# Two heads in row halves of TensorE, and a 32x32 block inverse in 32x32 array tiles, in the middle phase of an encoder layer

## The chip, the cores and the metric

One Trainium2 chip, one core. The metric is device time in microseconds of one launch of the whole layer; lower is better. The core has a matrix engine (TensorE, PE in the profile, with PEld for its weight loads), VectorE (DVE), ScalarE (ACT), GpSimd (POOL), SyncE (SP, which issues transfers here) and 16 DMA engines.

## The reference, cut to what matters

One encoder layer runs on two groups of tokens, 2048 and 256 long, with width 1024. Half of the heads are attention heads (8 of 64 columns), half are RWKV-7 heads (8 of 64), and a feed-forward part follows.

```python
h = rmsnorm(x, g_norm1) * (1.0 + sc1) + sh1
p = h @ w_in
attn = attention_mixer(p[..., :ATTN_IN], ...)      # dilated windows (128,1), (512,4), (2048,16)
rw = rwkv7_mixer(p[..., ATTN_IN:], ...)            # forward + backward scan
x = x + gt1 * (concat([attn, rw]) @ w_out)
x = x + gt2 * (square(relu(h2 @ w_ff1)) @ w_ff2)
...
def _rwkv_step(state, inp):
    w, kk, b, k, v, r = inp
    sa = einsum('dbhvk,dbhk->dbhv', state, kk)
    state = state * w[..., None, :] - sa[..., :, None] * b[..., None, :] + v[..., :, None] * k[..., None, :]
    y = einsum('dbhvk,dbhk->dbhv', state, r)
```

Attention needs, for each block of 128 queries and 128 to 256 keys, the scores `q @ k.T` of each head, a bias, an exponential and the product with the values. The scan is not run token by token: the kernel cuts it into chunks of 64 tokens, and in each chunk a 64x64 triangular matrix (made of products of the keys) has to be inverted before the state can be carried on.

## The kernel before, in words

The layer has three phases. `phase_a` (L292) is the input projection and what prepares the heads, `phase_b` (L1097) holds attention and the scan together, and `phase_c` (L1926) is the output projection with the feed-forward part. The change touches `phase_b` alone, beside two cost functions of the planner that it uses.

**Who sets the order.** In `phase_b` the work is written as generators ("streams"), and a planner, `Pace` (its `drive` is at L243), draws from them one step at a time: always the stream whose next step could begin earliest by an estimate, less a priority. The estimates are cost functions: `pe` (L143) for TensorE, `dve` (L164) for VectorE, with fixed latencies between engines. Only the order of each engine's instructions comes out of it; on the chip each engine runs its own list in that order and waits on semaphores. Where the planner foresees a gap on TensorE it writes filler products into the list (`warm`, L95, called by `heat`, L1123: 384-column f16 products of the constant `bdh` that nobody reads), to keep the granted clock up. All recorded operations pass one helper, so nearly every row of the profile says L117, and rows are told apart by their tiles' names.

**The scan.** Two neighbouring heads share one pass `c` of 128 partitions (head 0 in partitions 0 to 63, head 1 in 64 to 127), and there are four passes. For each pass and direction `d` (0 forward, 1 backward), 36 chunks are taken in "units" of eight (the short sequence: of four), 40 units in all. For a unit:

- `load_stream` (L1178) loads `kr` and `bk`. `prod_stream` (L1190) makes the key products: for four chunks at a time and one head after the other, a product over that head's 64 partitions, four chunks of head 0 into one PSUM bank `pb`, four of head 1 into another. `mask_stream` (L1212) copies them to SBUF as `x`, `gate_stream` masks them.
- `unit_prep` (L1294) inverts. The two diagonal 32x32 blocks of each head's 64x64 matrix are inverted together (four blocks for the two heads), as one block-diagonal 128x128 matrix per chunk: five levels, each one or two f16 products for every chunk of the unit, then one refinement and the off-diagonal block in split precision (`h` and `l` are the high and the low f16 part). Its left operands must be 128x128 with zeros off the diagonal: the copies `e`, `eof` live in zeroed tiles (`e32`, `eof`), and `spread` (L1313) is a VectorE multiply of a compact 128x(chunks x 32) tile by a mask into a 128x1024 tile (`mb`, `mbl`). `prep_stream` (L1857) runs one unit per direction at a time.
- `late_load` (L1239) and `late_gate` (L1252) bring the rest for half a unit: `rc`, the values into `uv`, and the transposed, weighted `bk` (which stays in SBUF from the first load until then).
- `pair_chain` (L1425) is the recurrent chain, 144 steps (4 passes x 36 chunks), both directions and both heads in one step. Each step runs five groups of four products on TensorE (`pc`), with ACT (`rr`, `uv`), POOL (`sw`) and DVE (`uv`) between them.

**Attention.** `attention` (L1561) cuts each pass into 50 blocks, 200 in all. `block` (L1601) yields a job: scores into a PSUM bank `ps` (two banks), a VectorE pass `p<-ps,tb` per head that adds the bias and takes the minimum, exponential on ACT, transposes `pt`, product with values into `pb`. Both heads' scores come from one product over all 128 partitions: the keys stand in `kz` (L1173), which has one half per head with the other head's partitions zeroed, so 2 x 256 columns are moved. For the windows of dilation 4 and 16 the keys and queries are read with that stride. At most six blocks are in flight.

PSUM has eight banks here: three `pb`, two `ps`, two `pc`, one `pt`.

## Time and profile before

| | us |
|---|---|
| median of 3 runs (4226.86 to 4237.39) | 4229.41 |
| the profiled execution | 4239.46 |
| its span, first to last instruction | 4237.6 |
| `phase_a`, until the first `pb` product | 0 to 1073 |
| `phase_b` | 1073 to 2361 |
| `phase_c` | 2361 to 4238 |

Two things help in reading it. An f32 product leaves two records in the trace (an f32 transpose and an f16 product one), so "x8" of `pb<-kr,bk` are four products. And a record's duration contains the way through the array, about 170 to 270 ns that overlap with the records behind it; what a product costs its neighbours is read from start to start in the timeline.

### The profile page before, as it was taken

How to read it: one execution, taken by the hardware profiler on the slowest of the kernel's cores; microseconds unless marked ns; L12 is line 12 of the kernel's file. 1: busy time of each engine (PE TensorE's matmuls, PEld its weight loads, DVE VectorE, ACT ScalarE, POOL GpSimd, SP SyncE). 2: the span in 40 equal slices, each digit the busy share in tenths (PEclk: the TensorE clock that was granted, in tenths of full speed). 3: DMA queues.
4: the chain of work that ended last, by engine and by line, in shares of the span. 5: the costliest groups of instructions: out<-in, count | busy, mean ns of one | idle time of the engine just before them, and what ended most of it. 6: DMA issues, size and time to landing. Idle time of an engine off the chain costs nothing.

```text
span 4237.6 us, 76554 instructions
## 1 busy us (share of the span) xinstructions
PE 4035.7 (95%) x29994; PEld 3339.5 (79%) x29994; DVE 2606.8 (62%) x5429; ACT 1754.5 (41%) x4301; POOL 1484.1 (35%) x1471
## 2 busy tenths in 40 slices
PE   8989999998899999999999799999999999999997
PEld 5878789888566666666666588889999888889997
DVE  4898788788668768767667354444444464444445
ACT  5556556555565566566465322121221221112221
POOL 2553431211645645645544443112121141112123
PEclk9999999999899899899799899999999999999999
DMA  6566565454433323324222444111111141111112
GB/s 228 205 224 224 173 201 191 152 171 153 145 79 94 106 69 93 110 71 109 83 75 55 155 145 154 41 40 48 42 44 42 53 167 40 40 40 43 48 41 80
DMA packets 341674, 452.57 MB, mean 107 GB/s; under 512 B 152384, under 2 KB 237376, under 8 KB 340288
## 3 DMA queue, kind: packets, MB, share of 16 engines
q1 hardware_dynamic: 340480, 446.98, 32.8%
q8 instruction: 236, 3.87, 0.4%
q14 instruction: 126, 1.03, 0.1%
q10 hardware_dynamic: 832, 0.69, 0.1%
HBM read 319.90 MB, written 127.68 MB: 106 GB/s over the span
## 4 chain that ended last, share of the span: by engine, by line
PE 54%; DVE 4%; issue 1%; ACT 1%; POOL 1%; DMA 0%; POOLq 0%; SPq 0%; DVEq 0%; ACTq 0%
PE p L117 42%; PE pb L117 5%; PE pc L117 3%; PE ps L117 3%; PE pt L117 1%; DVE mb L117 1%; DVE m L117 0%; DMA mx<-scr_mix 0%; DVE uv L117 0%; DVE mc L117 0%; DVE t L117 0%; POOL ya L117 0%; POOL x L117 0%; DVE w L117 0%; DVE p L117 0%
## 5 line engine op out<-in xcount | busy, mean ns | idle before, releaser
L117 DVE TENSOR_TENSOR z<-z 128x384 f32<-128x384 f32 x192 | 190.2, 991 | 591.1 <-ACT gh L117 591.1
L117 DVE TENSOR_TENSOR ya<-ya,p 128x512 f32<-128x512 f32 x540 | 363.9, 687 | 277.5 <-PE p L117 276.5
L117 PE MATMUL pin<-hi,whi 128*128 128x386 f32 (+3 forms) x1512 | 499.4, 330 | 16.6 <-ACT praw L325 8.9
L117 PE MATMUL p<-hi,mh 128*128 128x384 f32 x1536 | 513.3, 334 | 0.0
L117 PE MATMUL p<-hi,ml 128*128 128x384 f32 x1536 | 513.2, 334 | 0.0
L117 PE MATMUL p<-lo,mh 128*128 128x384 f32 x1536 | 513.0, 334 | 0.0
L117 PE MATMUL pin<-hi,wlo 128*128 128x386 f32 (+3 forms) x1512 | 484.6, 320 | 6.3 <-POOL wlo L117 5.1
L117 PE MATMUL pin<-lo,whi 128*128 128x386 f32 (+3 forms) x1512 | 484.0, 320 | 1.2 <-DVE lo L117 1.2
L117 PE MATMUL p<-xn,gh 128*128 128x512 f32 x1152 | 458.9, 398 | 0.0
L117 PE MATMUL p<-mx,gh 128*128 128x512 f32 x1152 | 458.1, 398 | 0.5 <-DVE ya L117 0.5
L117 PE MATMUL p<-mx,gl 128*128 128x512 f32 x1152 | 452.1, 392 | 0.0
L117 POOL TENSOR_TENSOR xn<-x,mx 128x1024 fp32r<-128x1024 f32 x64 | 152.8, 2407 | 653.7 <-ACT mx L117 653.7
L117 ACT ACTIVATE mx<-x 128x1024 fp32r<-128x1024 f32 x64 | 64.3, 1052 | 694.6 <-PE p L117 694.6
L117 POOL TENSOR_TENSOR ml<-x,mh 128x1024 fp32r<-128x1024 f32 x64 | 153.8, 2403 | 556.1 <-ACT mh L117 556.1
L117 PEld LDWEIGHTS pin<-hi,whi 128*128 128x128 f32 x1512 | 292.2, 193 | 30.3 <-ACT praw L325 9.8
L117 PEld LDWEIGHTS pin<-hi,wlo 128*128 128x128 f32 x1512 | 292.6, 193 | 9.3 <-POOL wlo L117 7.0
L117 PEld LDWEIGHTS pin<-lo,whi 128*128 128x128 f32 x1512 | 293.3, 194 | 5.5 <-DVE lo L117 2.7
L117 PEld LDWEIGHTS p<-hi,mh 128*128 128x128 f32 x1536 | 288.3, 188 | 1.5
L117 PEld LDWEIGHTS p<-lo,mh 128*128 128x128 f32 x1536 | 288.3, 188 | 1.3
L117 PEld LDWEIGHTS p<-hi,ml 128*128 128x128 f32 x1536 | 288.3, 188 | 0.0
L117 PE MATMUL ps<-kz,q 128*128 128x512 f32 (+2 forms) x400 | 272.7, 775 | 0.8 <-DVE st L117 0.6
L117 PEld LDWEIGHTS p<-mx,gh 128*128 128x128 f32 x1152 | 215.8, 187 | 56.5 <-DVE ya L117 0.9
(303 smaller groups left out, 8895.8 us busy)
## 6 DMA issues: line engine op xcount, KB each, us to landing
x<-wff SPq DMA_DIRECT2D x128, 512.0 KB
whi<-scr_wp SPq DMA_DIRECT2D x54, 512.0 KB
wlo<-scr_wp SPq DMA_DIRECT2D x54, 512.0 KB
raw<-wada SPq DMA_DIRECT2D x83, 256.0 KB
scr_kr<-kr SPq DMA_DIRECT2D x48, 384.0 KB
scr_bk<-bk SPq DMA_DIRECT2D x48, 384.0 KB
x<-xp SPq DMA_DIRECT2D x32, 512.0 KB
kr<-scr_kr SPq DMA_DIRECT2D x32, 512.0 KB
```

Source lines behind the costliest of these rows:

```text
L117: return f(out, *a, **k)
```

## The change

Six edits, all for `phase_b`:

1. **Key products.** `prod_stream` takes two `pb` banks at once and alternates the heads chunk by chunk, so that each product over partitions 0 to 63 is followed by one over 64 to 127.
2. **Scores.** `kz` loses its zeroed halves. Each head's scores are a product over its own 64 partitions, into a bank of its own, so a block takes both `ps` banks.
3. **Inverse.** `spread` and its masks go. `blocks` makes, for each chunk, four products of 32x32 blocks, block q from partitions 32q to 32q+31 to output partitions 32q to 32q+31 (for the off-diagonal block to those of the other block of the head). The operands stay compact.
4. **Two units in flight** per direction: four `prep` and four `low` streams instead of two, with four sets of tiles; `NX` 6 instead of 5 and `NLATE` 4 instead of 3.
5. **Buffers.** `bk` is dropped after the key products (`NBK` 2), and `late_load` loads it again in halves as `bkl`. In `uv` the head becomes the outer index, and `sw` is two tiles.
6. **The planner's numbers.** Scores and key products count half (`mm2`), a 32-row f16 product n/6 + 2.5 ns, a VectorE transpose at 0.87 elements per ns.

```diff
@@ Pace.pe
-    def pe(self, f):
-        def cost(out, a, b=None, *_, **k):
+    def pe(self, f, share=1.0):
+        def cost(*z, **k):
+            t, c = whole(*z, **k)
+            return t * share, c
...
-                return max(26.0, n / 2.4 + 3), n * rows
+                return (n / 6.0 + 2.5 if m == 32 else max(26.0, n / 2.4 + 3)), n * rows
@@ phase_b
+        mm2 = pace.pe(nc.tensor.matmul, 0.5)
...
-        NKR, NBK, NX, NH, NLATE, NY = 1, 3, 5, 3, 3, 4
+        NKR, NBK, NX, NH, NLATE, NY = 1, 2, 6, 3, 4, 4
...
-        kz = cp.tile([128, 2, NT], FT, name="kz")
-        for hd in range(2):
-            nc.gpsimd.memset(kz[64 - 64 * hd:128 - 64 * hd, hd], 0.0)
+        kz = cp.tile([128, NT], FT, name="kz")
@@ prod_stream
-                    for hd in range(2):
-                        pr = slice(64 * hd, 64 * hd + 64)
-                        yield room("pb", NPB), "P"
-                        ps, turn = pbank([128, 4, 128])
-                        for n in range(4):
-                            mm(ps[:, n], bk[pr, n0 + n, :], kr[pr, n0 + n, :], start=True, stop=True)
...
+                    yield room("pb", NPB), room("pb", NPB - 1), "P"
+                    u[n0, 0], u[n0, 1] = pbank([128, 4, 128]), take(psB, [128, 4, 128], FT, "pb", NPB)
+                    for n in range(4):
+                        for hd in range(2):
+                            pr = slice(64 * hd, 64 * hd + 64)
+                            mm2(u[n0, hd][0][:, n], bk[pr, n0 + n, :], kr[pr, n0 + n, :], start=True, stop=True)
@@ late_load
+                    yield room(f"bkl{d}", 1), "S"
+                    h["bkl", d] = take(su, [128, 4, 128], FT, f"bkl{d}", 1)
+                    dma_(h["bkl", d][0], S["bk"][c, d, :, n0:n0 + 4, :])
@@ unit_prep
-            def spread(c32, mask, name):
-                z = su.tile([128, 8, 128], FH, name=name, bufs=1)
-                tt(z[:, :nn].rearrange("p n (b t) -> p n b t", b=4), c32[:, :nn, None, :].to_broadcast([128, nn, 4, 32]),
-                   mask[:, None].to_broadcast([128, nn, 4, 32]), OP.mult)
-                return z
...
+            def blocks(ps, w, swap, *pairs):
+
+                for n in range(nn):
+                    for z, (a, b) in enumerate(pairs):
+                        for q in range(4):
+                            r, o = slice(32 * q, 32 * q + 32), slice(32 * (q ^ swap), 32 * (q ^ swap) + 32)
+                            mm(ps[o, n, 0:w], a[r, n], b[r, n], start=z == 0, stop=z == len(pairs) - 1)
...
-                    for n in range(nn):
-                        mm(ps[:, n, 0:16], mb[:, n], xs[:, n], start=True, stop=True)
+                    blocks(ps, 16, 0, (mc, xs))
...
                 vtr(fl(mc), fl(t))
-                if li < 4:
-                    mb = spread(mc, bd32, f"mb{d}")
@@ attention, block
-                    yield room("ps", 2), qk
-                    ps, turn = bank([128, 2, 256], "ps", 2)
-                    mm(ps[:, :, :nk], q[:, qs], kz[:, :, ks], start=True, stop=True)
+                    yield room("ps", 2), room("ps", 1), qk
+                    ps, turns = zip(bank([128, 256], "ps", 2), take(psB, [128, 256], FT, "ps", 2))
+                    for hd in range(2):
+                        pr = slice(64 * hd, 64 * hd + 64)
+                        mm2(ps[hd][:, :nk], q[pr, qs], kz[pr, ks], start=True, stop=True)
@@ prep_stream and its call
-            for u in units[d::2]:
+            for u in units[d::4]:
...
-            pace.add(prep_stream(d), "prep", lambda d=d: prog[1, d] + BT["prep"])
-            pace.add(low_stream(d), "low", lambda d=d: prog[1, d] + BT["low"])
+            for k in (d, d + 2):
+                pace.add(prep_stream(k), "prep", lambda d=k: prog[1, d] + BT["prep"])
+                pace.add(low_stream(k), "low", lambda d=k: prog[1, d] + BT["low"])
```

What moves on the engines is read from the order of the instructions. Three places matter. In each row stand the operation, output tile and operands, and the output's shape; the number behind a name is that of the buffer, and "x4" are four equal instructions in a row.

TensorE, the key products of four chunks, before: `pb_15542` takes head 0 and `pb_15552` head 1.

```order
L117 MATMUL pb_15536<-t1_15461,e3201_11132 128x16
L117 MATMUL pb_15542<-kr_15417,bk_15418 128x128 x4
L117 MATMUL pb_15552<-kr_15417,bk_15418 128x128 x4
L117 LDWEIGHTS mb1_15483
L117 MATMUL pb_15564<-xs1_15549,mb1_15483 128x16
```

And now, in the same kind of place (`pb_11698` is head 0, `pb_11699` head 1; behind them follow blocks of the inverse, now 32x16):

```order
L117 MATMUL pb_11660<-xs0_11607,mc0_11566 32x16
L117 MATMUL pb_11698<-kr_11489,bk_11490 128x128
L117 MATMUL pb_11699<-kr_11489,bk_11490 128x128
L117 MATMUL pb_11698<-kr_11489,bk_11490 128x128
L117 MATMUL pb_11699<-kr_11489,bk_11490 128x128
...
L117 LDWEIGHTS e3201_11132
L117 MATMUL pb_11722<-t1_11618,e3201_11132 32x16
```

The heads now alternate (the pair stands four times; two are left out), and what was one 128x16 product with its weight load is a run of 32x16 products, each with a weight load of its own.

TensorE, scores, with what stands between two blocks of attention; before, one product per block (`ps_17330`, `ps_17336`):

```order
L117 MATMUL pc_16869<-x_16323,uv_15940 64x64 x2
L117 MATMUL ps_17330<-kz_11157,q_16831 128x2x128
L117 MATMUL ps_17336<-kz_11157,q_16831 128x2x128
L117 MATMUL pb_17340<-ptb_17310,vx_17141 64x128 x2
L117 MATMUL pt_17343<-ident_58,p_17299 128x128 x2
```

Now two products per block, one per head and bank, with the next block behind other work:

```order
L117 MATMUL ps_22912<-kz_11165,q_21892 128x128
L117 MATMUL ps_22913<-kz_11165,q_21892 128x128
L117 MATMUL pc_21582<-uv_19661,bt0_20079 64x64 x2
L117 MATMUL pc_21582<-uv_19661,bt1_20144 64x64 x2
L117 MATMUL pc_21582<-x_18958,uv_19661 64x64 x2
L117 MATMUL pc_21582<-x_19582,uv_19661 64x64 x2
L117 MATMUL pt_22931<-ident_58,p_22885 128x128 x2
L117 MATMUL ps_22940<-kz_11165,q_21892 128x128
L117 MATMUL ps_22941<-kz_11165,q_21892 128x128
```

Before, two blocks could stand back to back, since each needed one of two banks; now the second needs both banks that the first has just filled.

VectorE, one level of the inverse in both directions (`mc0`, `mc1`: the transposed inverse so far), before:

```order
L117 SCALAR_TENSOR_TENSOR t0_18104<-pb_18415,t0_18104 128x16x8
L117 STREAM_TRANSPOSE mc0_18440<-t0_18104 128x256
L117 TENSOR_TENSOR mb0_18442<-mc0_18440,bdh_11125 128x1024
L117 TENSOR_TENSOR xs1_18457<-pb_18429,lvl_11121 128x128
L117 TENSOR_TENSOR t1_18411<-t1_18411,xs1_18457 128x128
```

And now:

```order
L117 SCALAR_TENSOR_TENSOR t0_21763<-pb_21857,t0_21763 128x64x2
L117 STREAM_TRANSPOSE mc0_21900<-t0_21763 128x256
L117 TENSOR_TENSOR xs0_21938<-pb_21904,lvl_11121 128x128
L117 SCALAR_TENSOR_TENSOR t0_21763<-pb_21940,t0_21763 128x32x4
L117 STREAM_TRANSPOSE mc0_21983<-t0_21763 128x256
```

The 128x1024 multiplies are gone. Counted over the whole order, `phase_b` has 5184 f16 products of the inverse before and 20736 after, 576 key products in both, 200 score products before and 400 after, and 371 fillers before and 238 after. VectorE has 280 instructions fewer (the `spread`s), SP 72 loads of `bkl` more and four of `kz` fewer, POOL two large memsets of `kz` fewer; ACT keeps its number. The shape of array tile that TensorE's products use (128x128, 128x64, 64x128, 64x64, 32x128, 32x32) changes from one product to the next 1591 times before and 1940 times after.

## The prediction

> **What bounds the kernel now.** I looked first at the busy time by stage. The columns are busy time and instructions of TensorE, its weight loads, VectorE, ScalarE and GpSimd, then the granted TensorE clock, the share of the DMA engines and GB/s.

> ```profile
> 0.00:1073.00 1073.00, 978.79 (x5608) 853.28 (x5609) 854.35 (x1370) 607.22 (x1232) 365.68 (x365) 0.95 0.56 193
> 1073.00:2361.00 1288.00, 1224.07 (x15315) 859.52 (x15313) 905.26 (x2840) 749.45 (x2435) 654.56 (x881) 0.93 0.32 88
> 2361.00:4238.00 1877.00, 1832.88 (x9073) 1626.73 (x9072) 847.23 (x1219) 397.82 (x634) 463.90 (x225) 0.99 0.21 70
> ```

> The change lies in the middle stage, 1288 us. TensorE is busy for 1224 us of it, 95%; VectorE for 70%, ScalarE 58%, GpSimd 51%. Next the waits of TensorE in that stage: total, times, longest.

> ```profile
> PE pb L117 <- DVE bdh L117: 11.1, 1, 11.1
> PE pb L117 <- DVE xs L117: 8.9, 14, 1.4
> PE pc L117 <- DVE uv L117: 7.4, 8, 1.7
> ```

> The longest kind is a single start-up wait, and 1288 - 1224 = 64 us are idle in all. So TensorE bounds the stage, and its groups by form are what has to be priced (count, busy us, mean ns):

> ```profile
> L117 PE MATMUL pb<-kr,bk 64*128 64x128 f32 x1152 | 155.1, 295 | 0.9 <-DMA bk<-scr_bk 0.5 <-ACT x L117 0.2 <-DVE mph L117 0.2
> L117 PE MATMUL ps<-kz,q 128*128 128x512 f32 x192 | 139.2, 814 | 0.1
> L117 PE MATMUL ps<-kz,q 128*128 128x256 f32 x128 | 72.4, 666 | 0.6 <-DVE st L117 0.6
> L117 PE MATMUL pb<-bdh 128*128 128x384 f16 x251 | 62.7, 370 | 11.1 <-DVE bdh L117 11.1
> L117 PE MATMUL ps<-kz,q 128*128 128x384 f32 x80 | 61.1, 854 | 0.1
> L117 PE MATMUL pc<-bdh 128*128 128x384 f16 x120 | 29.2, 357 | 0.0
> ```

> Key products take 155 us, scores 139.2 + 72.4 + 61.1 = 272.7 us, fillers 62.7 + 29.2 = 91.9 us. Fillers are work that nobody reads, so TensorE has about 64 + 92 = 156 us of slack, in small pieces.

> **The change part by part.** Prices come from the timeline of TensorE, from start to start (start us, us until the last record's end, what, records).

> ```profile
> 1639.72 1.16 PE L117 MATMUL pb<-kr,bk 64*128 64x128 f32 x8 [0.18 <-ACT x L117]
> 1640.80 0.45 PE L117 MATMUL pc<-uv,x 128*64 128x64 f32 x8
> ...
> 1848.79 2.17 PE L117 MATMUL ps<-kz,q 128*128 128x512 f32 x2
> 1850.78 0.36 PE L117 MATMUL pb<-t,e 128*128 128x16 f16 x8
> ```

> *Key products.* Four products of one head hold TensorE for 1640.80 - 1639.72 = 1.08 us, and 1152/8 = 144 such groups make 155.5 us, which is the row's 155.1. The new order pairs a product of partitions 0 to 63 with one of 64 to 127. Do the two run side by side? Before, such neighbours met only where a group of head 0 was followed at once by one of head 1:

> ```profile
> 1741.61 3.00 PE L117 MATMUL pb<-kr,bk 64*128 64x128 f32 x32
> 1744.54 0.19 PE L117 MATMUL pb<-mph,mb 128*128 128x32 f16 x1
> ```

> Four groups took 2.93 us instead of 4 x 1.08 = 4.32: at the three seams work of both halves overlapped. If every pair overlaps, 72 groups of both heads take 1.08 us each, and 155.1 - 77.8 = 77 us go. Ends: 0 and -77; I take **-70**, near the seams' row, since a group now needs two free `pb` banks.

> *Scores.* Half of 272.7 us would go, were there not a part that doesn't shrink, the load of the weights ahead of the first product. For that the first and the last record of one group of key products:

> ```profile
> 1639.72 0.37 PE L117 MATMUL pb<-kr,bk 64*128 64x128 f32 x1 [0.18 <-ACT x L117]
> ```

> ```profile
> 1640.60 0.27 PE L117 MATMUL pb<-kr,bk 64*128 64x128 f32 x1
> ```

> The first is 0.10 us longer. With 200 blocks (400 records, two each) 20 us stay, and (272.7 - 20)/2 = 126 us is the most that can go. The row at 1848.79 has keys read with a stride and takes 1.99 us; one of the same 512 columns read without a stride takes 0.96 (below, 1660.92). What makes strided reads slow no row shows, so whether they halve is open. Ends: 0 and -126; I take **-105**.

> *Inverse.* 5184 f16 products become 20736 of a quarter of the array each. What one costs now, and what TensorE shows for products in separate corners:

> ```profile
> 1656.94 0.19 PE L117 MATMUL pb<-mph,mb 128*128 128x32 f16 x1
> ...
> 1657.25 0.35 PE L117 MATMUL pb<-t,e 128*128 128x32 f16 x8
> ...
> 1660.92 1.12 PE L117 MATMUL ps<-kz,q 128*128 128x512 f32 x2
> 1661.88 0.60 PE L117 MATMUL pt<-ident,p 128*128 128x128 f32 x4
> ...
> 1667.49 0.36 PE L117 MATMUL pb<-t,e 128*128 128x16 f16 x8 [0.36 <-DVE t L117]
> 1667.78 0.45 PE L117 MATMUL pc<-uv,bt 128*64 128x64 f32 x8
> ```

> ```profile
> 1642.19 0.27 PE L117 MATMUL pc<-rr,m 64*64 64x64 f32 x1
> ```

> ```profile
> 1642.19 0.27 PE L117 MATMUL pc<-rr,m 64*64 64x64 f32 x2
> ```

> Twelve products lie between 1656.94 and 1657.25, 26 ns each, so the inverse costs 5184 x 26 = 135 us. The last two fences are windows from 1642.185, 10 and 15 ns long: the second product, in the other corner of the array, starts less than 0.01 us after the first, and the two together still take 0.27. If four in four corners follow each other at 7 ns (an estimate, somewhat under that 0.01 us), a set takes 28 to 29 ns: 150 us, **+15**. Below nothing it can hardly go, since each tile still moves the columns that the full array moved. The other end is one at a time at 26 ns, 20736 x 26 = 539 us, +404. I take the corner's row, because it has the same layout: separate input partitions, separate output partitions, one bank.

> [...]

> *Changes of tile shape* go from 1591 to 1940. At 1667.49 eight f16 products should take 8 x 26 = 0.21 us and the next shape begins after 0.29: 0.08 us each, so 349 x 0.08 = 28, **+29** with rounding up. If the 0.10 us of a fresh weight load comes on top each time, +63.

> *Score banks.* A block now takes both banks, so the next one's scores wait for VectorE to read both heads:

> ```profile
> L117 DVE CUSTOM_DVE_ANT_0 p<-ps,tb 128x256 f32<-128x256 f32 x192 | 73.2, 418 | 39.4 <-PE ps L117 28.5 <-ACT ptb L117 3.7 <-PE pt L117 2.3
> L117 DVE DVE_READ_ACCUMULATOR2_ANT st<- 128x1 f32 x384 | 31.5, 82 | 0.0
> ```

> That is 2 x (418 + 82) = 1.0 us and some 0.4 us of hand-over. By the order and these prices, other TensorE work of less than 1.4 us stands between two blocks in 20 of 198 cases. At up to 0.75 us each: **+15**, ends 0 and +20. Behind the waiting score product everything on TensorE queues, the chain's next group first.

> *VectorE* loses 280 multiplies:

> ```profile
> L117 DVE TENSOR_TENSOR mb<-mc,bdh 128x1024 f16<-128x1024 f16 x128 | 106.4, 831 | 4.4
> L117 DVE TENSOR_TENSOR mbl<-tpl,bdh 128x1024 f16<-128x1024 f16 x32 | 28.8, 898 | 0.1
> L117 DVE TENSOR_TENSOR mb<-mph,bdh 128x1024 f16<-128x1024 f16 x32 | 24.8, 775 | 1.1
> L117 DVE TENSOR_TENSOR mb<-tph,bdh 128x1024 f16<-128x1024 f16 x32 | 24.0, 749 | 0.0
> L117 DVE TENSOR_TENSOR mb<-mc,bdh 128x512 f16<-128x512 f16 x32 | 20.9, 652 | 1.1
> ```

> These alone are 205 us of 905, but VectorE isn't the bound; it can only shorten TensorE's 64 us of idling, so I count 0, ends -20 and 0. *Fillers* fall by 133, at 91.9/371 = 0.25 us each 33 us; they stand where the plan sees TensorE idle, so 0, ends -33 and 0. *Loads*: SP issues 72 more of 256 KB, 18.9 MB, while the DMA engines are 32% busy, and `bkl` has one buffer per direction, so later loads queue behind its wait; they run up to three halves ahead of the chain, and I count 0. If that cover went, the chain would wait. POOL's lost memsets stood at the stage's start, beside the wait for `bdh` (11 us at most): 0.

> **The sum.** -70 - 105 + 15 + 29 + 15 = -116 us. The profiled execution took 4239.46 us (span 4237.6), so it becomes 4123; the median of the runs, 4229.41, lies 10 us lower, so I predict **4113 us**. Since TensorE is the bound and about 1000 us of its real work stay, this case's own range is 4050 to 4170.

> **The rivals.**

> *Short products queue (slower).* Each 32x32 product costs TensorE 26 ns however many corners are free: +404 instead of +15, 4113 + 389 = 4502 us. For it: no row shows more than two records that start together. Against: the two `rr,m` starts. It decides where it eats the 116 us: spread over 20736 products these are 5.6 ns each, so at 7 + 5.6 = 12.6 ns per product the gain is gone. [...] Chance 0.12.

> *Something else takes over.* TensorE is relieved, but the order is fixed by estimates, and the recurrent chain waits on four engines in every step:

> ```profile
> 1658.06 0.45 PE L117 MATMUL pc<-uv,x 128*64 128x64 f32 x8
> ...
> 1664.69 0.47 PE L117 MATMUL pc<-uv,x 128*64 128x64 f32 x8
> ```

> Steps here follow at 6.6 us; 144 of them take 955 us, against 1172 forecast for the stage. So the chain alone doesn't bind, but with attention and inverse held between its groups half of the gain may be lost: 4229 - 58 = 4171 us. Chance 0.20.

> *Strided scores don't halve.* The -105 becomes 0: 4218 us, no change that can be told. Chance 0.06.

> *The halves never run side by side*, the change doesn't do what it says: 4113 + 70 + 105 = 4288 us, slower. The seams speak against it. Chance 0.04.

> **How the numbers follow.** The forecast has 0.58, the rivals 0.12, 0.20, 0.06 and 0.04. About 0.3%, 13 us, is what a measurement here can tell. Faster: 0.58 + 0.20 = 0.78. Same: 0.06. Slower: 0.12 + 0.04 = 0.16. The range leaves out the two slower cases; at the top it reaches past 4218 to 4230, and at the bottom to 4035, where the ends -77, -126, 0 and -33 meet the +29 and +15: -192, so 4037.

> **What would show it.** Right: `kr,bk` about 78 us busy, `ps` about 150, the f16 products of the inverse some 28 ns per set of four, TensorE still the busiest engine of a stage near 1170 us, and waits `PE ps <- DVE st` of 10 to 20 us. Wrong: sets of four at 50 ns or more; strided `ps` pairs still near 2 us; a stage whose TensorE is idle for over 150 us; or a granted clock well below 0.93, since fewer fillers and narrower products may count for less in whatever grants it.

## The result, and the profile after

The change made the kernel slower: 4261.3 us (4251.1 to 4270.58, five runs) against 4232.87 us (4226.86 to 4239.16, five runs) of the kernel before beside it, ratio 1.0065 with a 95% interval of 1.004 to 1.0089. The forecast was 4113 us, with a range up to 4230.

First the stages of the changed kernel, in the columns of the prediction's first fence (busy time and instructions by engine, granted TensorE clock, DMA share, GB/s):

```profile
0.00:1073.00 1073.00, 979.36 (x5695) 854.09 (x5696) 856.93 (x1377) 611.09 (x1240) 362.46 (x371) 0.96 0.57 197
1073.00:2382.00 1309.00, 1205.67 (x31047) 881.48 (x31045) 696.21 (x2554) 745.59 (x2428) 613.66 (x874) 0.79 0.35 100
2382.00:4259.00 1877.00, 1833.50 (x9072) 1627.36 (x9072) 846.67 (x1219) 397.55 (x634) 463.93 (x225) 0.99 0.21 70
```

With these cuts only the middle stage moved, from 1288 to 1309 us. TensorE is busy there for 18 us less and idle for 103 us instead of 64, and its granted clock fell from 0.93 to 0.79. The page's clock row (40 slices of the span) and its row of fetched instructions (packets, MB, share), before:

```profile
PEclk9999999999899899899799899999999999999999
...
q8 instruction: 236, 3.87, 0.4%
```

and after, where slices 11 to 22 are the middle stage:

```profile
PEclk9999999998588797789768899999999999999999
...
q8 instruction: 359, 5.88, 0.6%
```

TensorE's groups after, for those of the prediction's second fence:

```profile
L117 PE MATMUL pb<-kr,bk 64*128 64x128 f32 x1120 | 108.9, 348 | 3.8 <-DMA kr<-scr_kr 3.3 <-issue 0.3
L117 PE MATMUL ps<-kz,q 64*128 64x256 f32 x384 | 93.3, 559 | 0.6 <-DVE st L117 0.6
L117 PE MATMUL ps<-kz,q 64*128 64x128 f32 x256 | 52.8, 488 | 1.5 <-DVE st L117 1.2
L117 PE MATMUL pb<-bdh 128*128 128x384 f16 x152 | 41.0, 374 | 0.8 <-ACT x L117 0.8
L117 PE MATMUL ps<-kz,q 64*128 64x192 f32 x160 | 40.3, 587 | 0.0
L117 PE MATMUL pc<-bdh 128*128 128x384 f16 x63 | 13.9, 329 | 0.0
```

Key products fell from 155 to 109 us and scores from 273 to 186 us, and that at a lower clock. So the row halves do run side by side. TensorE's waits after (total, times, longest):

```profile
PE pb L117 <- issue: 50.1, 51, 2.7
PE pc L117 <- issue: 5.4, 9, 2.0
PE pc L117 <- DVE uv L117: 4.7, 13, 0.9
PE ps L117 <- DVE st L117: 1.9, 6, 0.6
```

"Issue" is a wait for nothing that the profile shows; before, it ended none of TensorE's idle time in this stage. How the two new things meet is seen in one place of the timeline (start, us to the last record's end, what, records, idle time before):

```profile
1519.75 0.36 PE L117 MATMUL pb<-xs,mc 32*32 32x16 f16 x32
1520.05 0.34 PE L117 MATMUL pb<-bdh 128*128 128x384 f16 x1
1520.32 0.20 PE L117 MATMUL pb<-t,e 32*32 32x16 f16 x5
1521.45 0.35 PE L117 MATMUL pb<-t,e 32*32 32x16 f16 x27 [0.93 <-issue]
```

Five products into a group of 32, TensorE has no instruction for 0.93 us. The stage rows for the 13.7 us ahead of 1521.3 and behind it show what this costs:

```profile
1507.60:1521.30 13.70, 12.51 (x480) 9.34 (x479) 8.82 (x33) 8.60 (x31) 3.34 (x7) 0.99 0.42 103
1521.30:1535.00 13.70, 12.98 (x251) 10.02 (x251) 3.86 (x17) 5.11 (x19) 2.27 (x4) 0.51 0.26 64
```

A pause of 0.93 us is followed by 13.65 us at half clock: if all of TensorE's work takes twice as long there, some 6.5 us more are gone.

**A ledger for the stage.** The clock's records hold only 1.0 and 0.5 (72 records in the trace of before, 104 in that of after), in steps of 3.413 us. I take half of the time at 0.5 in which TensorE was busy as lost. That is an upper bound: in after, 32 products of 32x16 take 0.22 us from the first start to the last at 0.5 and 0.20 at 1.0 (medians of 44 and 72 groups), while eight records of key products in before take 1.66 and 0.88 (10 and 69 groups). Busy time less that loss is "work at full clock", so that what is taken too much as loss is missing from the work. "By issue" is the part of the idle time whose waits the profile puts down to issue. Stage = work + loss + idle, in us, of one profiled execution each:

| kernel | time, median | ratio to before, 95% | stage | idle (by issue) | at half clock | lost | work |
|---|---|---|---|---|---|---|---|
| before | 4232.87 | | 1288 | 64 (0) | 170 | 82 | 1142 |
| after | 4261.3 | 1.0065 [1.004, 1.0089] | 1309 | 103 (55) | 537 | 248 | 958 |
| keys | 4227.01 | 0.9984 [0.997, 0.9998] | 1275 | 106 (0) | 200 | 94 | 1075 |
| scores | 4295.98 | 1.016 [1.0135, 1.0186] | 1366 | 92 (0) | 584 | 276 | 998 |
| keys_scores | 4222.76 | 0.9979 [0.9967, 0.9992] | 1276 | 113 (0) | 403 | 186 | 977 |
| inverse_only | 4370.22 | 1.0321 [1.0277, 1.0365] | 1433 | 84 (44) | 447 | 212 | 1137 |
| before_q | 4333.99 | 1.0252 [1.022, 1.0285] | 1384 | 76 (26) | 294 | 141 | 1167 |
| before_h | 4320.84 | 1.0216 [1.0197, 1.0234] | 1380 | 47 (3) | 313 | 153 | 1180 |
| after_fill | 4303.51 | 1.0168 [1.0144, 1.0192] | 1353 | 90 (57) | 303 | 138 | 1125 |
| after_padscores | 4285.8 | 1.0117 [1.0096, 1.0138] | 1336 | 97 (47) | 322 | 148 | 1091 |
| after_one | 4301.23 | 1.0167 [1.0138, 1.0196] | 1343 | 132 (78) | 473 | 209 | 1003 |
| after_s0 | 4279.7 | 1.0125 [1.0089, 1.0161] | 1314 | 129 (79) | 385 | 170 | 1015 |
| before_s0 | 4243.53 | 1.0033 [1.002, 1.0046] | 1290 | 58 (0) | 147 | 71 | 1161 |
| keys_s0 | 4215.29 | 0.9964 [0.9952, 0.9977] | 1262 | 88 (0) | 172 | 77 | 1097 |
| keys_scores_s40 | 4207.6 | 0.9945 [0.993, 0.996] | 1259 | 99 (0) | 302 | 144 | 1016 |
| keys_scores_s0 | 4200.94 | 0.9934 [0.9912, 0.9957] | 1251 | 95 (0) | 262 | 123 | 1032 |
| keys_scores_sm60 | 4218.98 | 0.9968 [0.9952, 0.9984] | 1266 | 90 (0) | 273 | 132 | 1045 |

The change took 184 us of work away, more than the 116 forecast. Idle time gave 39 us back and the clock 166 us; 39 + 166 - 184 = 21, the stage's 21 us.

Two things limit how finely the rows can be compared. All stages are cut at 1073 us, where the first `pb` product of before starts; in the other runs it starts between 1059 and 1073 us (after: 1061). From that product on the stage takes 1288 us before and 1321 after, and work, loss and idle time change by -178, +168 and +43; in keys the work falls by 59 instead of 67. And the profiled execution isn't always near the median: it lies 22 us above it for scores, 16 above for inverse_only, 12 below for after_s0. So differences under some 15 us between two rows say nothing.

### The profile page after: what moved, and what is told of

Its sections match the earlier page's. It is cut to its first block, busy times and chain, and to the rows that moved or that the text cites. A ratio compares the mean times of both kernels' runs of the same rounds, so it can differ in the third digit from the quotient of the medians.

```text
span 4259.2 us, 108144 instructions
## 1 busy us (share of the span) xinstructions
PE 4018.5 (94%) x45813; PEld 3362.9 (79%) x45813; DVE 2399.8 (56%) x5149; ACT 1754.2 (41%) x4301; POOL 1440.1 (34%) x1469
## 3 DMA queue, kind: packets, MB, share of 16 engines
q8 instruction: 359, 5.88, 0.6%
## 4 chain that ended last, share of the span: by engine, by line
PE 66%; DVE 3%; issue 3%; ACT 2%; POOL 1%; DMA 1%; SPq 0%; POOLq 0%; ACTq 0%; DVEq 0%
PE p L117 42%; PE pb L117 12%; PE pc L117 7%; PE ps L117 4%; PE pt L117 3%; POOL x L117 0%; DMA mx<-scr_mix 0%; DVE w L117 0%; ACT p L117 0%; DMA kr<-scr_kr 0%; POOL ya L117 0%; DVE uv L117 0%; DVE p L117 0%; DVE m L117 0%; POOL ysq L117 0%
## 5 line engine op out<-in xcount | busy, mean ns | idle before, releaser
L117 DVE TENSOR_TENSOR z<-z 128x384 f32<-128x384 f32 x192 | 189.9, 989 | 590.0 <-ACT gh L117 590.0
L117 DVE TENSOR_TENSOR ya<-ya,p 128x512 f32<-128x512 f32 x540 | 363.9, 687 | 277.9 <-PE p L117 276.7
L117 PE MATMUL pin<-hi,whi 128*128 128x386 f32 (+3 forms) x1512 | 499.0, 330 | 15.8 <-ACT praw L329 10.2
L117 PE MATMUL p<-hi,mh 128*128 128x384 f32 x1536 | 513.3, 334 | 0.0
L117 PE MATMUL p<-hi,ml 128*128 128x384 f32 x1536 | 513.2, 334 | 0.0
L117 PE MATMUL p<-lo,mh 128*128 128x384 f32 x1536 | 513.0, 334 | 0.0
L117 PE MATMUL pin<-hi,wlo 128*128 128x386 f32 (+3 forms) x1512 | 483.6, 320 | 6.4 <-POOL wlo L117 5.1
L117 PE MATMUL pin<-lo,whi 128*128 128x386 f32 (+3 forms) x1512 | 482.8, 319 | 0.7 <-DVE lo L117 0.7
L117 PE MATMUL p<-xn,gh 128*128 128x512 f32 x1152 | 458.9, 398 | 0.0
L117 PE MATMUL p<-mx,gh 128*128 128x512 f32 x1152 | 458.1, 398 | 0.5 <-DVE ya L117 0.5
L117 PE MATMUL p<-mx,gl 128*128 128x512 f32 x1152 | 452.1, 392 | 0.0
L117 POOL TENSOR_TENSOR xn<-x,mx 128x1024 fp32r<-128x1024 f32 x64 | 152.8, 2407 | 653.4 <-ACT mx L117 653.4
L117 ACT ACTIVATE mx<-x 128x1024 fp32r<-128x1024 f32 x64 | 64.3, 1051 | 694.4 <-PE p L117 694.4
L117 POOL TENSOR_TENSOR ml<-x,mh 128x1024 fp32r<-128x1024 f32 x64 | 153.8, 2403 | 556.3 <-ACT mh L117 556.2
L117 PEld LDWEIGHTS pin<-hi,whi 128*128 128x128 f32 x1512 | 291.9, 193 | 29.1 <-ACT praw L329 11.4
L117 PEld LDWEIGHTS pin<-hi,wlo 128*128 128x128 f32 x1512 | 291.9, 193 | 9.5 <-POOL wlo L117 7.1
L117 PEld LDWEIGHTS pin<-lo,whi 128*128 128x128 f32 x1512 | 292.9, 194 | 4.8 <-DVE lo L117 1.9
L117 PEld LDWEIGHTS p<-hi,mh 128*128 128x128 f32 x1536 | 288.3, 188 | 1.6
L117 PEld LDWEIGHTS p<-lo,mh 128*128 128x128 f32 x1536 | 288.3, 188 | 1.3
L117 PEld LDWEIGHTS p<-hi,ml 128*128 128x128 f32 x1536 | 288.3, 188 | 0.0
L117 PEld LDWEIGHTS p<-mx,gh 128*128 128x128 f32 x1152 | 215.8, 187 | 56.4 <-DVE ya L117 0.9
L117 PEld LDWEIGHTS p<-mx,gl 128*128 128x128 f32 x1152 | 216.5, 188 | 54.2
```

What stands on the lines that cost most here:

```text
L117: return f(out, *a, **k)
```

## The experiments

**What does the clock count?** My first theory was the area of the array in use, since the inverse's 32x32 tiles use a sixteenth each; the rivals were busy time and rows in use. The area theory's 2800 columns per window were an estimate from the traces of before and after: counted by area, with 0.44 ns a column (see below), 39 of their 43 full-clock windows that were filled to under 30% were followed by half clock, 11 of 66 of 30 to 40%, and none of 444 above (2800 columns are 36%).

*probe* adds about 300 us of products ahead of the stage's work, between full f32 products:

```diff
+        for _ in range(130):
+            nc.tensor.matmul(pz[:, 0:128], cmat[0:32], cmat[0:32], start=True, stop=True)
...
+        for _ in range(130):
+            nc.tensor.matmul(pz[0:64, 0:128], cmat[0:64, 0:64], cmat[0:64], start=True, stop=True)
...
+        for _ in range(1100):
+            nc.tensor.matmul(pz[:, 0:16], lw, eye32[:, 0:16], start=True, stop=True)
```

> Adds about 300 us of products that nobody reads at the start of the middle stage; the result is unchanged. Seven segments of some 28 us, each of one kind of product, with full 128x128 f32 products between them. Columns are counted per 3.413 us window of the clock's records, weighted with the share of the 128x128 array that the tile covers (the area). Theory (the granted clock follows area, threshold near 2800 full columns per window): f32 32x128 tiles stay below (2048): clock 0.5. f32 64x128 tiles (4096): clock 1.0. f32 64x64 tiles (2048): 0.5. f16 128x128 with 32 columns every 26 ns (about 4200): 1.0. The same with 16 columns (2100): 0.5. f16 sets of four 32x32 tiles with 32 columns (about 1050 by area): 0.5. Rival, the clock counts busy time: all seven at 1.0. Rival, the clock counts rows of the array in use: 64x64 f32 (4096 by rows) and the 32x32 sets (4200 by rows) at 1.0, the 32-row f32 and the 16-column f16 at 0.5.

The stage rows inside six of its segments, in this order: f32 tiles of 32 rows by 128 columns, 64 by 128, 64 by 64, then f16 products of 32 columns, of 16 columns, and 32x32 sets:

```profile
1103.00:1150.00 47.00, 47.00 (x224) 47.00 (x222) 0.00 (x0) 0.00 (x0) 0.00 (x0) 0.50 0.00 1
1182.00:1211.00 29.00, 29.00 (x260) 28.88 (x260) 0.00 (x0) 0.00 (x0) 0.00 (x0) 1.00 0.00 1
1241.00:1269.00 28.00, 28.00 (x259) 27.95 (x257) 0.00 (x0) 0.00 (x0) 0.00 (x0) 1.00 0.00 1
1299.00:1329.00 30.00, 27.16 (x1053) 26.57 (x1050) 0.00 (x0) 0.00 (x0) 0.00 (x0) 1.00 0.02 4
1362.00:1389.00 27.00, 25.96 (x952) 25.59 (x949) 0.00 (x0) 0.00 (x0) 0.00 (x0) 0.51 0.02 4
1424.00:1534.00 110.00, 35.45 (x3712) 32.34 (x3712) 0.00 (x0) 0.00 (x0) 0.00 (x0) 0.50 0.02 4
```

In the first five TensorE is busy for over 90% of the time, at 0.50, at 1.00 and at 0.51, so it is not busy time. A 64x64 tile keeps the clock as a 64x128 tile does, and a 32x128 tile, which has the same area as 64x64, doesn't; so it is not area: my theory fell here. What fits all six is the share of the 128 rows times the share of time in which columns move. Twelve 384-column f16 products take 2.04 us in this trace, 0.44 ns a column; products that start every 28 ns move 32 columns in 14 ns and 16 in 7. So in these segments 25% of the rows' time had 0.50 (f32) and 0.51 (f16), and 50% had 1.00, f32 and f16 alike.

The traces of before and after fit this count. I counted the columns in their 760 windows of 3.413 us in the middle stage, every column with its full-clock time (0.44 ns, and 0.88 in a record of an f32 product: 260 records of 128 columns take 29.2 us in the probe's 64x128 segment), and two products that use the same rows in different columns of the array once:

| rows' time filled, by this count | windows at full clock | followed by half clock | windows at half clock | followed by half clock |
|---|---|---|---|---|
| under 30% | 22 | 22 | 51 | 51 |
| 30 to 40% | 42 | 26 | 114 | 101 |
| 40% and more | 489 | 2 | 42 | 4 |

By area the full-clock windows divide as well (above), so what decides against it is the probe. At half clock the columns themselves take longer, key products 1.66 us instead of 0.88 for eight records; so what counts as 40% took some 75% of the time of such a window, an estimate from these two times.

By this count a score product with its zeros holds all rows; two row halves side by side hold them too, but only half as long. The zeros were work that nobody reads, and they kept the clock up as the fillers do: with them the changed kernel's stage had 0.88 instead of 0.79 (*after_padscores* below), with 528 more fillers 0.89 (*after_fill*).

The same probe gave the second finding unasked. The rows of the timeline where the 32x32 segment starts:

```profile
1420.58 2.42 PE L1198 MATMUL ps<-eye 32*32 32x32 f16 x264
1425.83 1.22 PE L1198 MATMUL ps<-eye 32*32 32x32 f16 x128 [2.83 <-issue]
1429.57 1.22 PE L1198 MATMUL ps<-eye 32*32 32x32 f16 x128 [2.52 <-issue]
```

After 264 products TensorE runs 128 in 1.22 us and then has none until 3.74 us after the last start. I read this as the supply of instructions, from the packets of instructions: after, 5.88 MB in 359 packets are 16.4 KB each, and the 123 packets more than before fall into the middle stage (244 against 121), where the change adds 31,104 products and weight loads, 253 for each of them. The probe's segment runs 128 products with their loads, 256 instructions, per 3.74 us, 29 ns per product, where it ran the first 264, a little over twice as many, at 9 ns each. The trace of the DMA queue fits this in the changed kernel itself: of the 60 waits of over 0.15 us that issue ended in its stage, 58, with 54 of the 55 us, end 1.2 to 1.7 us after a packet of instructions has landed, as all 39 do in the probe; of the 80 waits ended by other engines or transfers 7 do.

*probe2* measures this by bursts of 16 to 128 sets of four tiles between 14 us of full products, then a long row of f32 tiles:

```diff
+        for n in (16, 32, 48, 64, 96, 128):
+            quad(n)
+            full(60)
+        quad(600, cmat, 4)
```

> Adds products nobody reads at the start of the middle stage; the result is unchanged. Bursts of 16, 32, 48, 64, 96 and 128 sets of four 32x32 f16 products (two instructions each, with the weight load), 60 full f32 products (14 us) between bursts; then 2400 f32 32x32 products of 4 columns (one instruction each), then 500 sets of f16 again. Theory (a block of 256 instructions per 3.74 us, one or two blocks fetched ahead): the bursts of 16 to 48 sets run through without idle time, at 7 to 9 ns per product; those of 96 and 128 sets stop for 2 to 3 us at a block's end; the long f32 row advances at 256 products per 3.74 us, 14.6 ns each, the f16 row at 128 per 3.74 us, 29 ns each. Rival, what is slow is the change of tiles or the weight load: the f32 row goes at 29 ns or slower as well, and the short bursts stop too.

Its timeline, bursts of 32, 48 and 64 sets, and two blocks of the f32 row:

```profile
1116.79 1.18 PE L1183 MATMUL ps<-eye 32*32 32x32 f16 x128
...
1131.50 1.32 PE L1183 MATMUL ps<-eye 32*32 32x32 f16 x144
1134.07 0.52 PE L1183 MATMUL ps<-eye 32*32 32x32 f16 x48 [1.26 <-issue]
...
1148.12 1.92 PE L1183 MATMUL ps<-eye 32*32 32x32 f16 x216
1152.76 0.45 PE L1183 MATMUL ps<-eye 32*32 32x32 f16 x40 [2.73 <-issue]
...
1228.34 1.88 PE L1183 MATMUL ps<-cmat 32*32 32x4 f32 x128 [2.78 <-issue]
1232.09 1.89 PE L1183 MATMUL ps<-cmat 32*32 32x4 f32 x128 [1.86 <-issue]
```

Bursts up to 128 products run through; from 192 on they stop, after 144 to 232 products. The f32 row missed my number: 58 ns per product, not 14.6. But each f32 product leaves two records, with a weight load each, and 128 records with their loads per 3.74 us are again the f16 row's rate.

**Each edit alone.** *keys* is before with edit 1 alone, *scores* with edit 2, *keys_scores* with both (their diffs are the `prod_stream` and the `kz` and `block` parts of the change), *inverse_only* has edits 3, 5 and 6 with one unit per direction.

> Before with edit 1 alone: key products of the two heads alternate in row halves. It adds no instructions and takes no row-columns away (1567 thousand columns weighted by the share of the rows in use, as before). Theory (the clock falls for a few windows after each stretch of about 1 us in which TensorE is idle, and neither the supply of instructions nor the rows change here): key products fall from 155 to about 80 us, a few more waits on VectorE cause a few more drops, clock 0.90 to 0.93, time 4160 to 4200 us, ratio 0.983 to 0.993. Rival, every us that TensorE saves comes back as half-clock time: 4225 to 4240 us, clock under 0.89. Rival, the two banks at once hold up other work: 4240 to 4270 us with waits for a pb bank.

> Before with edit 2 alone: scores in row halves, both score banks per block. Row-weighted columns fall by 162 thousand (the zeros of kz are no longer moved). Theory (idle stretches start half-clock stretches, fewer row-weighted columns make them longer): score products fall by about 100 us at the full clock, and 60 to 110 us come back as half-clock time: clock 0.85 to 0.88, 4200 to 4250 us. Rival, only the new waits count and the columns don't: clock 0.90 or more and 4130 to 4180 us. Rival, the two banks serialise the blocks: TensorE waits of over 40 us for VectorE's reads of the scores.

> Before, with key products and scores in row halves (edits 1 and 2) and the old 128x128 inverse. Area theory: TensorE's full-array columns of the stage fall from 1479 to 1299 thousand, in a stage that gets shorter, so the granted clock of the stage stays near 0.91 and the prediction's -70 and -105 arrive with +15 for the banks: about 4075 to 4140 us, ratio 0.963 to 0.978. Rival, the order with both banks and both halves is what costs the time: 4210 to 4260 us. Rival, instruction supply: the same short time as by the area theory, but with the clock at 0.93 or more.

> Before, with the inverse in 32x32 tiles, its buffers and the planner's numbers (edits 3, 5 and 6), one unit per direction in flight; keys and scores as before. Area theory: full-array columns fall from 1479 to 1353 thousand while the work does not get shorter, clock of the stage 0.86 to 0.89, 4280 to 4340 us, ratio 1.01 to 1.025. Rival, instruction supply: the after kernel's 50 us of idle time ended by issue are here too and the clock stays at 0.92 or more, 4270 to 4300 us. Rival, the inverse costs nothing by itself (the loss of after comes from keys and scores): 4220 to 4245 us with the clock at 0.93.

The rows of the stage, of keys,

```profile
1073.00:2348.00 1275.00, 1169.27 (x15248) 806.71 (x15246) 902.50 (x2835) 737.86 (x2429) 652.95 (x876) 0.92 0.32 87
```

of scores,

```profile
1073.00:2439.00 1366.00, 1273.60 (x15649) 951.77 (x15647) 900.81 (x2839) 756.67 (x2436) 650.36 (x881) 0.79 0.30 83
```

of keys_scores,

```profile
1073.00:2349.00 1276.00, 1163.35 (x15658) 854.95 (x15656) 906.87 (x2839) 748.39 (x2435) 653.09 (x881) 0.84 0.32 89
```

and of inverse_only:

```profile
1073.00:2506.00 1433.00, 1349.36 (x30771) 926.54 (x30771) 693.70 (x2555) 756.82 (x2435) 616.92 (x881) 0.84 0.34 94
```

Each loses in its own way. *keys* keeps its clock, as expected, but of 67 us of work saved 42 come back as idle time. Its waits tell on whom, the four longest:

```profile
PE pb L117 <- DVE xs L117: 15.2, 22, 1.7
PE pb L117 <- ACT ysq L117: 11.5, 7, 3.7
PE pb L117 <- DVE wz L117: 11.2, 9, 2.5
PE pb L117 <- DVE tpl L117: 8.1, 13, 1.1
```

A TensorE that is done sooner waits for VectorE's part of the same inverse (`xs`, `tpl`), and as much for ScalarE: over the stage the waits that VectorE ended grew by 20 us and those that ScalarE ended by 19. That is the prediction's second rival, with these two in the place of the chain. The 4160 to 4200 us of my theory were missed. The time fell in the range of this experiment's first rival, "every us comes back", but through idle time more than through the clock, which that rival had below 0.89.

*scores* saves the most work, 144 us, and loses 194 us to the clock: 25 stretches at half clock with 23 us on the mean, where before has 17 of 10 us. Without the zeros the half-clock stretches last longer, which fits the count above (152 of 165 half-clock windows under 40% were followed by another). The time, 4296, lies above every range that I gave; waits for the two banks, the last rival, come to 3 us. *keys_scores* missed too (4075 to 4140 expected, 4223 measured). Its time lies where the rival had it that blamed the order, but the ledger has 165 us of work gone, of which 104 came back through the clock and 49 as idle time. *inverse_only*, at 4370 also above all ranges, has next to no change in work (-5 us) and loses 130 us to the clock and 20 to idle, 44 of its idle us ended by issue.

**Is it the supply of instructions that makes the tiled inverse dear?** *before_nops* was meant to add the instructions without the tiles:

```diff
+            def more():
+                for _ in range(6):
+                    nc.tensor.nop(hint="x", nofuse=True)
...
                     mm(ps[:, n, 0:16], eh[:, n], sel[:, n], start=True, stop=True)
+                    more()
```

> Before, with six no-operation instructions on TensorE behind each of the 5184 products of the inverse: 31,104 more instructions, the number that the 32x32 tiles add, with no product, tile shape, operand or column changed. Theory (instructions reach TensorE at about 128 products with their weight loads, 256 instructions, per 3.74 us, as the segment of 32x32 products showed; a burst that runs faster starves, and the idle stretch drops the clock): idle time ended by issue of 30 to 70 us, clock 0.80 to 0.88, 4290 to 4400 us, ratio 1.015 to 1.04, near the 4370 of the kernel with the tiled inverse alone. Rival, the tiled inverse costs its time by its tile shapes, its buffers or its order: here 4230 to 4250 us, clock 0.92 or more and next to no idle time ended by issue.

It took 6092.87 us (ratio 1.4392, 1.437 to 1.4413) and tells nothing of the supply: products with six no-operations between them start 0.45 us apart, so one costs some 70 ns itself (their records stand 71 ns apart).

*before_q* and *before_h* answer better. They cut each product of before into its four 32x32 or two 64x64 diagonal blocks, from the same operands; the planner counts the parts as a quarter and a half, so that all other TensorE instructions stand in the same order as before:

```diff
-                    mm(ps[:, n, 0:16], eh[:, n], sel[:, n], start=True, stop=True)
+                    part(ps[:, n], slice(0, 16), 0, eh[:, n], sel[:, n], start=True, stop=True)
...
+            def part(ps, w, swap, a, b, **k):
+                for q in range(4):
+                    r = slice(32 * q, 32 * q + 32)
+                    o = slice(32 * (q ^ swap), 32 * (q ^ swap) + 32)
+                    mmt(ps[o, w], a[r, o], b[r], **k)
```

> Before with each 128x128 product of the inverse cut into its four 32x32 blocks on the diagonal, from the same operands: no other instruction, buffer, filler, plan or engine changes, 15,552 products and as many weight loads more on TensorE; the zeros off the diagonal are no longer multiplied. Theory (instructions come at 128 products with weight loads per 3.74 us; bursts starve, idle stretches start half-clock stretches): the work stays near 1144 us, idle time ended by issue rises from 4 to 40 to 80 us, half-clock loss from 82 to 150 to 220 us: 4310 to 4420 us, clock 0.82 to 0.88. Rival, the loss of the tiled inverse came from its buffers, the second load of the keys or the new plan: 4235 to 4265 us with under 15 us idle by issue. Rival, short tiles queue: the work itself grows by 50 us or more.

> The same with two 64x64 blocks instead of four 32x32: a third of the added instructions (5,184 products and weight loads), the same changes of tile shape around each group. Theory (supply of instructions): a group of eight chunks is 16 products, 0.47 us of supply, much of it covered by the instructions fetched ahead: idle time by issue 8 to 25 us, 4240 to 4300 us, and at most half of the loss with four blocks. Rival, the changes of tile shape cost the time: the same loss as with four blocks.

The stage of before_q,

```profile
1073.00:2457.00 1384.00, 1307.65 (x30824) 897.56 (x30823) 900.35 (x2835) 752.21 (x2433) 646.30 (x881) 0.89 0.31 82
```

and of before_h:

```profile
1073.00:2453.00 1380.00, 1332.63 (x20492) 930.00 (x20489) 898.40 (x2839) 751.80 (x2436) 649.94 (x881) 0.89 0.31 83
```

Supply alone is not it. With four tiles the time came as expected, but the 26 us more idle by issue and the 141 us lost at half clock stayed below the 40 to 80 and the 150 to 220 expected; and two tiles, with 3 us by issue, cost nearly as much, as the rival of the tile shapes had it, and missed the theory's 4240 to 4300. Common to both are 25 and 38 us more of work (a group of eight 16-column products, at the full clock and from start to start, takes 278 ns in one piece, 294 in four, 348 in two; medians of some 200 groups each), and 59 and 71 us lost to the clock. Why half clock grows that much with two tiles is open: the row-columns and the order are the same, and only the longer groups are seen. Such a group is thin in any form, 8 x 16 columns at 0.44 ns being 56 ns of its 278. Of the 138 us that inverse_only lost against the before beside it, some 100 come from the cutting itself, if the two add up; the rest would lie in its buffers and plan, which no run took apart further.

**Does activity buy the clock back?** *after_fill* puts one filler ahead of each group of the inverse, *after_padscores* takes the zeros back into `kz`, *after_one* undoes edit 4, and *after_s0* lets the planner fill smaller gaps. Their cores, in this order:

```diff
+                mm(flat[:, :384], bdh[:, 0].rearrange("p b t -> p (b t)"),
+                   bdh.rearrange("p a b t -> p (a b t)"), start=True, stop=True)
```

```diff
-                        mm2(ps[hd][:, :nk], q[pr, qs], kz[pr, ks], start=True, stop=True)
+                    mm(ps[:, :, :nk], q[:, qs], kz[:, :, ks], start=True, stop=True)
```

```diff
-            for u in units[d::4]:
+            for u in units[d::2]:
```

```diff
-job=-4, flight=6, AHEAD=10, SPARE=100, ENOUGH=5000)
+job=-4, flight=6, AHEAD=10, SPARE=0, ENOUGH=9000)
```

> After, with one more 384-column filler product ahead of each group of the inverse, 528 more that nobody reads: 83 us more work for TensorE at the full clock. Area theory: full-array columns rise from 1172 to 1375 thousand, the stage's clock from 0.79 to about 0.90, and the time falls in spite of the added work, to 4170 to 4230 us. Rivals (instruction supply, the new order, waits): nothing that costs time is taken away, so the time rises by up to 83 us, 4290 to 4345.

> After with the old score products over all 128 partitions, zeros included (NX 5 instead of 6 for the room). TensorE gets about 105 us more work at the full clock and 162 thousand more row-weighted columns. Theory: the stretches at half clock get shorter (clock 0.84 to 0.88 instead of 0.79) and some 40 to 80 us of the added work come back, 4280 to 4330 us. Rival, what the columns do to the clock is nothing (the starts of the drops are all that counts): clock 0.80 or less and 4360 us or more. Rival, the zeros paid for themselves altogether: 4265 us or less.

> After with edit 4 undone: one unit of the inverse per direction in flight instead of two; the plan then holds 371 fillers instead of 238. Theory (stage = work at the full clock + idle time + half of the time at half clock; idle stretches start the half-clock stretches): fewer groups of the inverse follow each other closely, so idle time ended by issue falls from 58 to some 40 us, and the added fillers shorten the half-clock stretches: clock 0.82 to 0.86, 4230 to 4275 us. Rival, the second unit in flight is what keeps TensorE fed, and without it the chain waits for the inverse: 4300 us or more with long waits of the chain's products. Rival, two units are the cause of the loss: 4170 us or less with idle time by issue under 20 us.

> After with the same planner numbers (SPARE 0, ENOUGH 9000): 405 fillers instead of 238. Theory: 167 fillers at 0.16 to 0.32 us (the higher end where the shape of the array tile changes around them) add 27 to 53 us and take 50 to 100 us off the 247 us lost at half clock, while the idle time ended by issue stays near 58 us: 4210 to 4255 us, clock 0.83 to 0.87. Rival, a filler costs what it gives: 4260 to 4300 us.

The stage of after_fill:

```profile
1073.00:2426.00 1353.00, 1263.24 (x31605) 876.94 (x31606) 697.82 (x2555) 745.82 (x2428) 614.80 (x876) 0.89 0.35 97
```

and of after_padscores:

```profile
1073.00:2409.00 1336.00, 1238.92 (x30776) 840.05 (x30774) 691.34 (x2555) 747.22 (x2434) 616.89 (x881) 0.88 0.36 99
```

In all four the loss at half clock falls, by 110, 100, 39 and 78 us against after's 248: activity buys the clock, whether by fillers or by zeros. None is faster. A filler between 32x32 groups cost 0.32 us (167 us of work for 528), twice the 0.17 us of fillers in a row, so that *after_fill* missed its 4170 to 4230 by over 73 us; it came out where the rivals had it (4290 to 4345), though the clock did rise to the 0.89 that the theory forecast. The zeros give back three quarters of what they cost (133 us of work, 100 of clock), within that theory's range. *after_one* missed its 4230 to 4275. Its 4301 us are those of the rival by which the second unit keeps TensorE fed, but the long waits of the chain's products that this rival named aren't there (`pc` waits for VectorE and ScalarE come to 12 us, against 11 in after); what grew is idle time by issue, to 78 us, so this doesn't come from the second unit. *after_s0* fell in its rival's range: 57 us of work and 24 more idle by issue against 78 of clock.

**The version that beats both.** The two edits without the tiled inverse have no supply problem (0 us idle by issue in keys_scores), and their gaps are such as fillers can cover. *keys_scores_s0* is keys_scores with the SPARE and ENOUGH of after_s0 (554 fillers instead of 326), *keys_scores_s40* and *keys_scores_sm60* have SPARE 40 and -60 (498 and 709 fillers), *keys_s0* has edit 1 alone, *before_s0* none. All fillers of these runs are products that nobody reads.

> Before with edits 1 and 2, and the planner allowed to put a filler where it foresees any gap of 163 ns (SPARE 0 instead of 100, ENOUGH 9000 instead of 5000): 554 fillers instead of 326, all read by nobody. Theory: 228 fillers at some 0.2 us add up to 46 us of work, fill 20 to 30 us of the 111 us that TensorE idled, and take 50 to 90 us off the 186 us lost at half clock: 4150 to 4200 us, clock about 0.90. Rival, a filler costs what it gives: 4215 to 4245 us.

> Before with edits 1 and 2 and SPARE 40: 498 fillers, between the 326 of SPARE 100 (4223 us) and the 554 of SPARE 0 (4201 us). Theory: between the two, 4195 to 4220 us, clock 0.87 to 0.90. Rival, the optimum lies at fewer fillers than 554: below 4195 us.

> Before with edits 1 and 2 and still more fillers, SPARE -60 instead of 0: 709 instead of 554 (326 without the new planner numbers). Theory: 155 more fillers add 31 us of work, fill some 10 us of the 93 us idle and take 20 to 50 us off the remaining 124 us of half-clock loss: 4175 to 4205 us, clock 0.91 to 0.94. Rival, the fillers now cost what they give or more: 4205 to 4235 us.

> Before with edit 1 alone and the same planner numbers (SPARE 0, ENOUGH 9000): 461 fillers instead of 340. Theory: 121 fillers add 24 us, fill 15 to 25 us of the 104 us idle and take 20 to 40 us off the 94 us lost at half clock: 4190 to 4220 us, clock 0.93 to 0.95. Rival, a filler costs what it gives: 4225 to 4240 us.

> Before with the planner numbers of the fastest version alone (SPARE 0, ENOUGH 9000): 504 fillers instead of 371. Theory (row halves and fillers need each other: the halves take TensorE's work away, the fillers keep the clock up over the gaps that this opens): here there are only 63 us idle and 82 us of half-clock loss to win from, 133 fillers add 27 us, so 4215 to 4240 us, above the 4201 of both edits with these numbers. Rival, the planner numbers alone make the gain: 4205 us or less.

The stage of keys_scores_s0:

```profile
1073.00:2324.00 1251.00, 1155.92 (x15837) 841.62 (x15837) 901.28 (x2835) 745.89 (x2431) 654.10 (x877) 0.90 0.32 89
```

Against keys_scores the fillers add 55 us of work and take 18 us of idle time and 63 us of loss: 4201 us, 0.9934 of before, just above the 4150 to 4200 expected. More fillers (4219, the rival's range) are worse, fewer (4208) no better, with edit 1 alone the gain is half as large (0.9964), and without the edits the fillers make the kernel slower (1.0033, 3.5 us above its range). Neither part is worth much alone; the gain is that of the two together.

## Why the prediction was wrong

**Key products, -70.** Right: -67 us of work in keys, and 155.1 us of records became 91.3 at nearly the same clock:

```profile
L117 PE MATMUL pb<-kr,bk 64*128 64x128 f32 x1120 | 91.3, 305 | 3.6 <-DVE m L117 1.4 <-DMA kr<-scr_kr 1.4 <-DVE tpl L117 0.3
```

**Scores, -105, and banks, +15.** Right in kind, too small in size. *scores* shows -144, of which some 11 are 66 fillers that fell away. Strided reads shrink as the others do: at the full clock a block of 2 x 256 takes 0.63 us without and 1.21 us with a stride, where one of 512 columns took 0.96 and 1.99 (timeline). The banks cost 1.9 us, in the wait row `PE ps <- DVE st` above.

**Inverse, +15, and shapes, +29.** About right as work: +25 in before_q for both together, and -5 in inverse_only, where the plan differs. Products of 32x32 follow at 7 ns as assumed, 32 in 0.22 us in the changed kernel.

**The step that failed** is the one from the terms to the sum: "Since TensorE is the bound and about 1000 us of its real work stay". It took the durations of a stage at 0.93 and booked the removed work as time. Three entries were missing; the first two are what the changed kernel lost by. The clock: the terms removed work that had held it up (the zeros, 133 fillers), and, together with the pauses of the next entry, +166 us followed; the prediction had put the fillers at 0 because they stand where TensorE idles, but there they held up the clock: 167 more of them took 78 us off the loss (after_s0). Supply: 31,104 more TensorE instructions were priced by what TensorE does with them and not by how they arrive, +55 us of idle time. The other engines at 0: true while TensorE is slower, untrue as soon as it isn't (42 us more idle in keys, half of it for VectorE). In the changed kernel itself this third entry didn't count: without the 55 us by issue its idle time is 48 us, under the 64 of before. With 64 us idle and 95% busy before, the stage was bound by TensorE only just.

The prediction's last line named "a granted clock well below 0.93, since fewer fillers and narrower products may count for less" as a sign of being wrong. It was the sign, but its reasons were only part of it. In the probe narrower tiles counted by their rows and not by their columns: 64x64 tiles had 1.00 as 64x128 tiles had, 32x128 tiles 0.50. Fillers count, but 167 more of them won back 78 of the 166 us (after_s0); the zeros of the scores, which the prediction saw as waste alone, were worth 100 (after_padscores). And the sign stood in no rival with a price: the slower side held the queueing of products at 4502 us and row halves that never run side by side at 4288, and no run showed either.

**How pause and clock work together.** In eight of these traces (before, after, the edits alone and together, after_fill, after_padscores), of 72 windows of 3.413 us at full clock in which TensorE was idle for 1.6 us or more, 68 were followed by half clock; with 0.8 to 1.2 us 44 of 103; with under 0.4 us 23 of 1764. Before has 17 half-clock stretches of 10 us on the mean, after 35 of 15 us. In 14 of the 34 that begin within after's stage most of the idle time in the 3.413 us ahead of the drop was ended by issue (in 12 by VectorE), in before in none of 16 (in 13 by VectorE).

What stays open: how much of after's 166 us is due to the pauses by issue and how much to the missing rows, since the two act on each other, how much of the 166 is only the upper bound of the count, and why two 64x64 tiles cost as much as four of 32x32.

## What to carry to other kernels

Before work is taken from a matrix engine whose clock depends on its activity, write the ledger of the stage as work, half-clock loss and idle time, and ask of every saving whether it also held up the clock: zeros and fillers may (here the zeros took 100 us off the loss, 167 fillers 78). Count instructions as well as columns: 32x32 products that follow at 7 ns in groups of 32 came at 29 ns in a long row. When the saved work opens pauses, fill them again: here the edits alone gave 0.2%, with more fillers 0.66%.
